# A hybrid convolution and state-space trunk: the input projection as a stage of its own, in seven block products

## The chip, the core and the metric

The kernel runs on one core of one Trainium2 chip. The metric is the device time of one execution in microseconds (us), lower is better. A core has a matrix engine (TensorE, PE in the profile; its weight loads are PEld), a vector engine (VectorE, DVE), an activation engine (ScalarE, ACT), GpSimd (POOL), and SyncE (SP), which here issues the transfers. The engines work on a memory on the chip with 128 partitions; matmul results go to an accumulator memory (PSUM) of eight banks of 512 float32 columns. Inputs, outputs and scratch tensors lie in device memory. Each engine runs its instructions in the order that was written for it.

## The reference

One layer over 1024 tokens of 1024 channels, all float32:

```python
h = layer_norm(x, ln_in_g, ln_in_b)
u = h @ w_in                      # 1024 x 9248 columns:
u_glu, z, xbc, dt_raw, gate_a, gate_b = split_in(u)
# u_glu 2x1024, z 2048, xbc 2048+2x512, dt 32, two gates of 1024
a, g = split(u_glu)
y_a = silu(layer_norm(causal_dwconv31(a * sigmoid(g)))) @ w_conv_out
xbc = silu(causal_dwconv4(xbc))   # x, B, C of the state-space scan
dt = softplus(dt_raw + dt_bias)
y = ssd_chunked(x, dt, -exp(a_log), B, C) + x * d_skip   # chunks of 128 tokens
y_b = rms_norm_by_group(y * silu(z)) @ w_ssm_out
mix = (sigmoid(gate_a) * y_a + sigmoid(gate_b) * y_b) @ w_o
h = layer_norm(ALPHA * h + mix)
gate, val = split(causal_dwconv3(h @ w_ffn_up))          # 2 x 2816 columns
h = layer_norm(ALPHA * h + (silu(gate) * val) @ w_ffn_down)
```

## The kernel before

Every matrix product is made of three float32r matmuls: both operands are split into a rounded part and a rest (`weights`, L144 to L153: ACT writes the rounded part at L149, DVE the rest at L150), and `mm3` adds rounded times rounded, rounded times rest and rest times rounded (L161 to L163). A tile of 128 columns over half of the tokens (512) and all 1024 input channels is `project`: eight k-steps of three matmuls, 24 in all, into one bank.

The tokens are worked on in two halves. For each half: `ln_in` normalises four row tiles of 128 tokens and transposes them to `hT`; `mixers` computes the projection columns and the two mixing branches; `combine` joins them; `out_proj` (for the second half `out_proj_pairs`) multiplies by `w_o` and applies the next LayerNorm.

`mixers` begins with the columns for dt and the first B and C (`first_columns`), turns dt into decays (`time_steps`), and then goes over four groups of heads. For a group it projects B, C and four x tiles with `conv4` on each (ACT copies the bank to `u`, one tap on ACT, three taps on DVE at L370, SiLU), computes z (`z_gate`, tokens on the partitions, L161 to L163 with `w_z`), projects the two GLU pairs of two channel tiles (`glu`), and runs the scan over four chunks of 128 tokens (`ssd_group`: transposes, the decay mask through POOL L473, PE L482, ACT L490 and L491 and DVE L507, the masked product L529, the state update). The 31-tap convolution of the two GLU tiles, 30 taps each on DVE at L415, is issued at a lower priority (`high_priority(offset=-1500)`). Small halo tiles carry the last tokens of the first half into the second. After the groups come the eight tiles of gate_a, kept in device memory; `combine` projects the eight tiles of gate_b in turn with the second half of the ssm output product (`w_sp`), does the LayerNorm of the convolution (`cc` to `sT`, POOL L611 to L624, DVE L618 to L631) and the product with `w_conv_out` (`w_co`).

The up projection works on all 1024 tokens at once, in a Winograd form of Strassen's scheme with seven block products for a pair of column tiles instead of eight. `ffn_blocks` forms the blocks and their sums from both halves of the tokens and of the channels. `up_first` computes the two products of the first tile that need only the first half of the tokens, for eight tiles ahead of the others and then interleaved with them, and keeps them in device memory; `up_rest` does the other five (12 matmuls each in `product`), and the weights' sums on DVE (`up_weights`, L823 to L829). The last stage is `down`.

The order on each engine is set by a list scheduler when the kernel is built: an instruction goes by program order shifted by the `offset` of the priority that it stands under, and by the time at which its inputs are expected; a tile waits until the buffer that it takes is free. Of the stages, tiles for weights have three buffers (`wst` for the loaded tile, `wsp` for its split), PSUM has four banks of kind `acc` (`bank(1)`) and four of kind `sm` (`bank(0)`), and two big tiles of 32 KB a partition hold hT, yT and mixT in turn.

Of the kernel before, what the change touches and what calls it, by code (L numbers as in the profile page):

```python
# [8 lines left out]
F32 = mybir.dt.float32  # L9
# [7 lines left out]
P = 128  # L17
D = 1024
# [10 lines left out]
EPS = 1e-5  # L29

# [25 lines left out]
def kernel(  # L56
# [37 lines left out]
    state_stack = ExitStack()  # L94
    statep = state_stack.enter_context(pool("states", side="right"))
    upper = statep.tile([P, P], F32, name="upper")
    make_upper_triangular(nc, upper, 1.0, diag=True)
    later = statep.tile([P, P], F32, name="later")
    make_lower_triangular(nc, later, 1.0, diag=False)
    ones = statep.tile([P, P], F32, name="ones")  # L100
    V.memset(ones, 1.0)
# [22 lines left out]
    a_log = statep.tile([P, HEADS], F32, name="a_log")  # L124
    dskip = statep.tile([P, HEADS], F32, name="dskip")
    u_halo = statep.tile([P, 24, 3], F32, name="u_halo")
    G.memset(u_halo, 0.0)
    v_halo = statep.tile([P, 8, KC - 1], F32, name="v_halo")
    G.memset(v_halo, 0.0)
    states = [statep.tile([P, HALF], F32, name=f"state{g}") for g in range(GROUPS)]  # L130
    dts = [statep.tile([P, 4, HEADS], F32, name=n) for n in ("dtv", "wds")]
    edc = statep.tile([P, 3, 4, HEADS], F32, name="edc")
    seg_mv = statep.tile([P, 4, P], F32, name="seg_mv")
    seg_st = statep.tile([P, 4, P], F32R, name="seg_st")
# [3 lines left out]
    first_scr = [dram.tile([2, P, HALF], F32, name=f"first_scr{j}") for j in range(NF)]  # L138
    act_scr = [dram.tile([P, T], F32, name=f"act_scr{j}") for j in range(NF)]
    c_scr = [dram.tile([8, P, HALF], F32, name=f"c_scr{i}") for i in range(2)]  # L140
    g_scr = [dram.tile([8, P, HALF], F32, name=f"g_scr{i}") for i in range(2)]
# [87 lines left out]
    def ln_in(hh):  # L229
        hT = big_tile(f"hT{hh}")  # L230
        with pool(f"lnin{hh}", side="right") as pl:
            first = hh == 0
            xts, gb = [], []
            with tc.high_priority(offset=6000):
                for t in range(4):
                    xt = pl.tile([P, D], F32, tag="x", bufs=4, name=f"x{hh}_{t}")
                    r0 = hh * HALF + t * P
                    SY.dma_start(xt, x[r0 : r0 + P, :])
                    xts.append(xt)
                    if first and t == 1:  # L240
                        gb = [row(pl, RW_ING, D, "in_g"), row(pl, RW_INB, D, "in_b")]
# [833 lines left out]
```

## Time and profile before

| | |
|---|---|
| time, median of 3 runs | 2039.81 us (2035.84 to 2040.16) |
| the profiled execution | 2041.08 us, its span 2039.3 us |
| mean granted TensorE clock | 0.996 |
| PE busy | 2000.0 us, 9296 matmul records |
| DVE busy | 1654.7 us, 2185 instructions |
| ACT / POOL busy | 973.0 us / 148.0 us |
| device memory | 279.81 MB moved, 137 GB/s on average |

"Busy" is the time in which at least one record of the engine was open. A matmul's record is longer than the distance to the next one, since matmuls overlap; so work on PE is priced by the distance between starts. Records on DVE overlap by some hundredths of a microsecond too. Rows of groups read: line, engine, operation, output from inputs, shapes, count, then busy time and the mean of one in ns, then idle time just before and what ended it. fp32 matmuls (the scan and the transposes) leave two records each.

### The profile page before, as it was taken

To read this page: it belongs to the slowest core of one execution; us is meant where nothing else is said; L and a number is where in the kernel's file an instruction comes from. 1 tells how busy PE (TensorE), PEld (TensorE's weight loads), DVE (VectorE), ACT (ScalarE), POOL (GpSimd) and SP (SyncE) were. 2 spreads that over 40 slices of the span, in tenths; PEclk is the share of its full clock that TensorE was granted. 3 is DMA by queue.
4 is the path that set the end of the run, shared out by engine and by line. 5 is a ranking of instruction groups with operands and counts; after the bars stand their busy time and mean duration, and the time that the engine had idled before them with its cause. 6 is when DMAs were issued, how large, how long until landed. Compare 5 with 4: busy or idle time off the path is not lost.

```text
span 2039.3 us, 24778 instructions
## 1 busy us (share of the span) xinstructions
PE 2000.0 (98%) x9296; PEld 1650.1 (81%) x9296; DVE 1654.7 (81%) x2185; ACT 973.0 (48%) x1392; POOL 148.0 (7%) x125
## 2 busy tenths in 40 slices
PE   7999999999999999999999999999999999999998
PEld 6888887888788888888888888877888888888886
DVE  7599999989766869999998976586888888853736
ACT  4465654556453356665454635354444444433231
POOL 2010101001400000100100130010000000000000
PEclk9999999999999999999999999999999999999999
DMA  6222223333436522222323353566454444464542
GB/s 218 93 69 88 86 94 104 99 103 114 158 121 213 209 88 77 90 84 76 126 88 104 109 171 128 195 217 217 155 164 157 164 165 156 160 227 149 209 159 83
DMA packets 95015, 279.81 MB, mean 137 GB/s; under 512 B 10800, under 2 KB 10800, under 8 KB 94896
## 3 DMA queue, kind: packets, MB, share of 16 engines
q1 hardware_dynamic: 94896, 278.24, 40.3%
q8 instruction: 73, 1.20, 0.2%
q14 instruction: 46, 0.38, 0.1%
HBM read 229.96 MB, written 48.23 MB: 136 GB/s over the span
## 4 chain that ended last, share of the span: by engine, by line
PE 69%; DVE 23%; issue 4%; DMA 2%; ACT 1%; SPq 0%; POOL 0%; DVEq 0%; ACTq 0%
PE acc L163 15%; PE acc L161 15%; PE acc L162 15%; DVE c L415 8%; PE sm L161 6%; PE sm L163 6%; PE sm L162 6%; DVE xbc L370 2%; PE acc L352 1%; PE sm L529 1%; PE sm L510 1%; DVE w_so L150 1%; DVE w_z L150 1%; DVE w_c L150 1%; PE sm L187 1%
## 5 line engine op out<-in xcount | busy, mean ns | idle before, releaser
L415 DVE SCALAR_TENSOR_TENSOR c<-v,pc,c 128x512 f32<-128x512 f32 x480 | 375.3, 805 | 7.2 <-ACT c L404 5.8
L473 POOL TENSOR_TENSOR au<-seg_mv,head_of 128x1024 fp32r<-128x1024 f32 x32 | 77.6, 2425 | 961.8 <-PE sm L482 728.8
L161 PE MATMUL acc<-hT,w_c 128*128 128x512 f32 x352 | 141.0, 400 | 0.0
L162 PE MATMUL acc<-hT,w_c 128*128 128x512 f32 x352 | 140.6, 399 | 0.0
L163 PE MATMUL acc<-hT,w_c 128*128 128x512 f32 x352 | 138.4, 393 | 0.0
L150 DVE TENSOR_TENSOR w_dn<-st_dn,w_dn 128x1024 fp32r<-128x1024 f32 x44 | 53.4, 1222 | 104.2 <-ACT w_dn L149 104.2
L370 DVE SCALAR_TENSOR_TENSOR xbc<-u,pc,xbc 128x512 f32<-128x512 f32 x144 | 109.8, 774 | 0.7 <-ACT xbc L368 0.5
L161 PE MATMUL sm<-h1s,w_s 128*128 128x512 f32 x264 | 103.5, 392 | 6.0 <-DVE fuv L848 3.1
L149 ACT CAST w_dn<-st_dn 128x1024 fp32r<-128x1024 f32 x44 | 46.0, 1053 | 131.6 <-PE sm L163 115.4
L162 PE MATMUL sm<-h1s,w_s 128*128 128x512 f32 x264 | 102.8, 389 | 0.0
L163 PE MATMUL sm<-h1s,w_s 128*128 128x512 f32 x264 | 102.1, 389 | 0.0
L162 PE MATMUL acc<-w_z,hT 128*128 128x512 f32 x256 | 100.8, 394 | 0.0
L161 PE MATMUL acc<-w_z,hT 128*128 128x512 f32 x256 | 100.8, 401 | 0.0
L163 PE MATMUL acc<-w_z,hT 128*128 128x512 f32 x256 | 100.7, 396 | 0.0
L149 ACT CAST w_c<-st_c 128x1024 fp32r<-128x1024 f32 x50 | 52.5, 1051 | 86.9 <-PE acc L163 66.2
L162 PEld LDWEIGHTS acc<-hT,w_c 128*128 128x128 f32 x352 | 66.1, 188 | 16.9 <-issue 3.8
L163 PEld LDWEIGHTS acc<-hT,w_c 128*128 128x128 f32 x352 | 66.1, 188 | 16.1 <-issue 2.6
L161 PEld LDWEIGHTS acc<-hT,w_c 128*128 128x128 f32 x352 | 66.1, 188 | 15.9 <-issue 2.6
L150 DVE TENSOR_TENSOR w_c<-st_c,w_c 128x1024 fp32r<-128x1024 f32 x47 | 60.6, 1289 | 20.2 <-ACT w_c L149 20.2
L163 PE MATMUL acc<-h1b,w_ue 128*128 128x512 f32 x176 | 68.5, 391 | 2.0 <-DVE w_ue L150 2.0
L161 PE MATMUL acc<-h1b,w_ue 128*128 128x512 f32 x176 | 68.7, 391 | 1.1 <-ACT s L807 0.7
L163 PE MATMUL sm<-h1b,w_s 128*128 128x512 f32 x176 | 69.2, 393 | 0.0
(312 smaller groups left out, 5741.8 us busy)
## 6 DMA issues: line engine op xcount, KB each, us to landing
st_c<-wcol SPq DMA_DIRECT2D x50, 512.0 KB, 3.5
st_dn<-wdown SPq DMA_DIRECT2D x44, 512.0 KB, 3.6
st_z<-wz SPq DMA_DIRECT2D x32, 512.0 KB, 3.4
st_wo<-wo SPq DMA_DIRECT2D x24, 512.0 KB, 3.9
st_ue<-wup SPq DMA_DIRECT2D x22, 512.0 KB, 4.1
ra<-wup SPq DMA_DIRECT2D x22, 512.0 KB, 3.8
rb<-wup SPq DMA_DIRECT2D x22, 512.0 KB, 3.5
act_scr<-fo SPq DMA_DIRECT2D x22, 512.0 KB, 2.7
```

What stands on the lines that cost most here:

```text
L149: A.copy(w[:, 0, :], st)
L150: (eng or V).tensor_tensor(out=w[:, 1, :], in0=st, in1=w[:, 0, :].bitcast(F32), op=ALU.subtract)
L161: TE.matmul(ps, wa(0), xa(0), start=start, stop=False, skip_group_check=more)
L162: TE.matmul(ps, wa(0), xa(1), start=False, stop=False, skip_group_check=more)
L163: TE.matmul(ps, wa(1), xa(0), start=False, stop=stop, skip_group_check=more)
L187: TE.transpose(pt[:, i * P : (i + 1) * P], src[:, (q + i) * P : (q + i + 1) * P], ident)
L352: TE.matmul(ps[:, ts], w[:, i, k * P : (k + 1) * P], hT[:, j, k, ts], start=n == 0 and k == 0, stop=n == 2 and k == KD - 1,)
L370: V.scalar_tensor_tensor(out=o, in0=u[:, k : k + HALF], scalar=pc[:, wc + k : wc + k + 1], in1=o, op0=ALU.mult, op1=ALU.add,)
L415: V.scalar_tensor_tensor(out=accs[i], in0=v[:, k : k + HALF], scalar=pc[:, wc + k : wc + k + 1], in1=accs[i], op0=ALU.mult, op1=ALU.add,)
L473: G.tensor_tensor(out=au, in0=seg_mv[:, c, :].unsqueeze(1).to_broadcast([P, 8, P]), in1=head_of[:, g, :].unsqueeze(2).to_broadcast([P, 8, P]),
L510: TE.matmul(po, CT[:, cs], S, start=True, stop=True)
L529: TE.matmul(py[:, hs], m[:, h, :], xs[:, hs], start=True, stop=True)
```

## The change

The columns of the input projection, all but z, are taken out of `mixers` and `combine` and computed over all tokens before the mixers, in the seven-product form of the up projection. `ln_in` is replaced by `in_blocks`, which normalises all eight row tiles and forms the blocks; `blocks` holds what `ffn_blocks` did. `columns` first computes the two early products of eight pairs (`lead_first`), closes the pool of the rows, and then goes over 28 pairs in a written order (GLU pairs, x, B with C, gates); `pair` computes a pair, and its convolution, GLU or sigmoid follows. The results, `xbc`, `v` and both gates over 1024 tokens, go to device memory, and the dt columns too (`time_columns`, five block products of 12). The 31-tap convolution of the first half of the tokens is done there; that of the second half is issued after the first mixers at an offset of -1500. The mixers read their tiles back. The blocks' first tile `b1` serves as `hT` for z of the first half; for the second, `rebuild` reads the normalised rows and transposes them. The tiles of the scan's states are opened only after the columns (`open_states`). The up projection uses the same `pair`: the first eight are led, the others compute all seven products in a row, with copies on ACT in place of some additions on DVE. The pair's loaded weights come from `wst` and no longer from a pool of their own.

```diff
-    def ln_in(hh):
...
-    def column(hh, hT, ct):
...
-    def first_columns(hh, hT, cts):
...
-    def time_steps(pl, hh, ps):
+    def time_steps(pl, hh):
         dtc = pl.tile([HEADS, HALF], F32, tag="yo", name=f"dtc{hh}")
-        A.activation(
-            out=dtc, in_=ps[:HEADS, :], func=AF.Identity, bias=pc[:HEADS, PC_DTB : PC_DTB + 1]
-        )
+        SY.dma_start(dtc, dt_scr[:, hh * HALF : (hh + 1) * HALF])
...
-    def conv4(pl, hh, ps, j):
+    def conv4(pl, j, u):
+        o = pl.tile([P, T], F32, tag="o", bufs=2, name=f"xo{j}")
...
+        A.activation(
+            out=o, in_=u[:, U0 : U0 + T], func=AF.Identity, scale=pc[:, wc + 3 : wc + 4]
+        )
         for k in range(3):
             V.scalar_tensor_tensor(
                 out=o,
-                in0=u[:, k : k + HALF],
+                in0=u[:, U0 - 3 + k : U0 - 3 + k + T],
...
+        SY.dma_start(xbc_scr[j], o)
+    def glu(i, ua, ug):
+        a, g = ua[:, U0 : U0 + T], ug[:, U0 : U0 + T]
+        A.activation(out=g, in_=g, func=AF.Sigmoid)
+        V.tensor_mul(a, a, g)
+        SY.dma_start(v_scr[i], a)
...
     def mixers(hh, hT):
-        pre = first_columns(hh, hT, (CT_DT, CT_B, CT_C))
         with pool(f"mixers{hh}") as pl:
-            time_steps(pl, hh, pre[0])
+            time_steps(pl, hh)
             for g in range(GROUPS):
...
+                tiles = []
+                for j in (*range(4 * g, 4 * g + 4), 16 + g, 20 + g):
+                    o = pl.tile([P, HALF], F32, tag="xbc", bufs=12, name=f"xbc{hh}_{j}")
+                    SY.dma_start(o, xbc_scr[j][:, hh * HALF : (hh + 1) * HALF])
+                    tiles.append(o)
                 zs = z_gate(pl, hh, hT, g)
-                vs = [(i, glu(pl, hh, hT, i)) for i in (2 * g, 2 * g + 1)]
-                done = ssd_group(pl, hh, g, xT, BT, CT, zs)
+                done = ssd_group(pl, hh, g, tiles[:4], *tiles[4:], zs)
...
+    def lead_first(qp, bl, js, src, n=1):
+        ws = {j: weights(src(j), f"ue{j}") for j in js}
+        pss = {j: bank(1) for j in js}
+        for h in range(n):
+            ts = slice(h * HALF // n, (h + 1) * HALF // n)
+            for q, block in enumerate(("b11", "b21")):
+                for j in js:
+                    product(
...
+                    for t in range(ts.start, ts.stop, HALF // 2):
+                        f = qp.tile([P, HALF // 2], F32, tag="f", bufs=4, name=f"f{j}{q}{t}")
+                        A.copy(f, pss[j][:, t : t + HALF // 2])
+                        SY.dma_start(first_scr[j][q][:, t : t + HALF // 2], f)
+    def pair(upp, bl, j, src_a, src_b):
+        led = j < LEAD
         with tc.high_priority(offset=2000):
+            r1 = wst.tile([P, D], F32, tag="st", name=f"ra{j}")
+            SY.dma_start(r1, src_a)
+            r2 = wst.tile([P, D], F32, tag="st", name=f"rb{j}")
+            SY.dma_start(r2, src_b)
+            ue = None if led else split_pair(wsp, r1, f"ue{j}")
...
+        ps, pz = bank(1), bank(0)
+        if led:
+            SY.dma_start(s, first_scr[j][0])
+            SY.dma_start(ua[:, e], first_scr[j][1])
+            product(ps, lambda i: w24[:, i, :HALF], bl["t2"], True)
+            V.tensor_tensor(out=u2, in0=s, in1=ps, op=ALU.add)
+            product(pz, lambda i: w3[:, i], bl["t3"], True)
+            product(ps, lambda i: w10[:, i, :HALF], bl["t1"], False)
+            V.tensor_tensor(out=ub[:, l], in0=s, in1=ps, op=ALU.add)
+        else:
+            product(ps, lambda i: ue[:, i, :HALF], bl["b11"], True)
+            A.copy(s, ps)
+            py = bank(1)
+            product(py, lambda i: ue[:, i, HALF:], bl["b21"], True)
+            V.tensor_tensor(out=ua[:, e], in0=s, in1=py, op=ALU.add)
+            product(ps, lambda i: w24[:, i, :HALF], bl["t2"], False)
+            A.copy(u2, ps)
+            product(pz, lambda i: w3[:, i], bl["t3"], True)
+            product(ps, lambda i: w10[:, i, :HALF], bl["t1"], False)
+            A.copy(ub[:, l], ps)
+        V.tensor_tensor(out=ub[:, l], in0=ub[:, l], in1=pz, op=ALU.add)
+        product(pz, lambda i: w10[:, i, HALF:], bl["t4"], False)
+        V.tensor_tensor(out=ub[:, e], in0=u2, in1=pz, op=ALU.add)
+        product(ps, lambda i: w24[:, i, HALF:], bl["b22"], False)
...
+    def columns(bl, tp_stack, qp):
...
+        for r in range(4):
+            order += [glus[2 * r], xs[2 * r], bcs[r], gates[2 * r], xs[2 * r + 1]]
+            order += [glus[2 * r + 1], gates[2 * r + 1]]
...
+        lead_first(qp, bl, range(3), first, 2)
+        for j in range(3, LEAD):
+            lead_first(qp, bl, (j,), first)
+        tp_stack.close()
+        with pool("columns") as pl:
+            for j, (kind_, i) in enumerate(order):
+                ua, ub = pair(pl, bl, j, wcol[srcs[j][0]], wcol[srcs[j][1]])
+                if kind_ == "g":
+                    glu(i, ua, ub)
+                    with tc.high_priority(offset=-300):
+                        conv31(pl, 0, (i,))
...
+                if j == LEAD:
+                    time_columns(pl, bl)
...
-    hT = ln_in(0)
-    yT = mixers(0, hT)
-    mixT = combine(0, hT, yT)
-    hT = ln_in(1)
+    bl = in_blocks(tp_stack.enter_context(pool("intrans")), qp)
+    columns(bl, tp_stack, qp)
+    in_stack.close()
+    open_states()
+    cvp = state_stack.enter_context(pool("conv", side="right"))
+    yT = mixers(0, bl["b1"])
+    with tc.high_priority(offset=-1500):
+        for i in range(0, 8, 2):
+            conv31(cvp, 1, (i, i + 1))
+    mixT = combine(0, yT)
+    hT = rebuild(1)
...
-    LEAD = 8
-    firsts_to(LEAD)
+    for j in range(LEAD):
+        lead_first(qp, bl, (j,), lambda j: wup[j])
...
     for j in range(NF):
-        firsts_to(LEAD + (j + 1) * (NF - LEAD) // (NF - 1))
-        up_rest(upp, bl, j)
+        up(upp, bl, j)
```

385 lines of the change are left out of this document (190 added, 195 removed).

## The prediction

> **What bounds the kernel now.** I read the page first, then the table of busy time by stretch, then the order of time on PE and DVE inside the stretches, and last the groups of instructions.
>
> ```profile
> span 2039.3 us, 24778 instructions
> PE 2000.0 (98%) x9296; PEld 1650.1 (81%) x9296; DVE 1654.7 (81%) x2185; ACT 973.0 (48%) x1392; POOL 148.0 (7%) x125
> ```
>
> PE idles 39 us of 2039, so PE work taken away is the only large thing to win. DVE is the next engine, with 385 us spare over the whole run. Where that spare time lies is in the stretches (columns: stretch, its length, busy time and count of PE, PEld, DVE, ACT, POOL, then the granted clock, the DMA share and GB/s):
>
> ```profile
> 0.00:39.00 39.00, 26.16 (x181) 25.22 (x182) 28.48 (x44) 14.21 (x29) 10.85 (x15) 1.00 0.70 242
> 39.00:500.00 461.00, 460.06 (x2185) 377.48 (x2186) 424.94 (x591) 265.50 (x424) 38.96 (x16) 1.00 0.29 94
> 500.00:691.00 191.00, 185.80 (x833) 152.84 (x832) 133.65 (x173) 77.39 (x103) 22.49 (x14) 0.98 0.50 171
> 691.00:1192.00 501.00, 500.54 (x2448) 414.20 (x2448) 463.62 (x647) 274.91 (x417) 38.62 (x16) 1.00 0.30 99
> 1192.00:1308.00 116.00, 115.44 (x505) 94.55 (x505) 73.61 (x86) 53.33 (x68) 22.41 (x14) 1.00 0.45 151
> 1410.00:1800.00 390.00, 386.93 (x1696) 318.83 (x1695) 334.53 (x387) 163.33 (x179) 4.08 (x41) 1.00 0.48 160
> 2015.00:2040.00 25.00, 15.25 (x68) 12.30 (x66) 21.01 (x40) 1.18 (x4) 0.00 (x0) 0.90 0.23 84
> ...
> 1003.00:1045.00 42.00, 41.54 (x200) 33.62 (x199) 42.00 (x57) 16.89 (x30) 4.81 (x3) 1.00 0.30 99
> ```
>
> 39 to 500 is mixers of the first half of the tokens, 691 to 1192 mixers of the second, 1192 to 1308 the second combine, 1410 to 1800 the up projection. In the two mixers PE is full, but DVE is already busy 92% (425 of 461, 464 of 501), and for a while all the time (42.00 of 42). The projection columns are what keeps PE full there, while DVE does the scan and the 31-tap convolution under them. The change takes exactly those columns out of there.
>
> **Prices.** Records overlap, so prices are start to start.
>
> ```profile
> 1542.58 0.39 PE L161 MATMUL acc<-h1b,w_ue 128*128 128x512 f32 x1
> ...
> 1545.07 0.39 PE L163 MATMUL acc<-h1b,w_ue 128*128 128x512 f32 x1
> ```
> ```profile
> 450.87 1.21 DVE L150 TENSOR_TENSOR w_gt<-st_gt,w_gt 128x1024 fp32r<-128x1024 f32 x1
> 452.00 2.73 DVE L415 SCALAR_TENSOR_TENSOR c<-v,pc,c 128x512 f32<-128x512 f32 x4
> 454.65 0.68 DVE L530 TENSOR_TENSOR t<-t,sm 128x512 f32<-128x512 f32 x1
> 455.25 0.68 DVE L495 TENSOR_TENSOR xs<-sm,dtv 128x512 f32<-128x512 f32 x1
> ...
> 1539.70 1.28 DVE L863 SCALAR_TENSOR_TENSOR fo<-fuv,pc,fo 128x1024 f32<-128x1024 f32 x1
> 1540.90 0.69 DVE L727 TENSOR_TENSOR w_s<-s,w_s 128x512 fp32r<-128x512 f32 x1
> ```
> ```profile
> 788.62 1.73 PE sm L529 x16
> ```
>
> A matmul of 512 columns costs 2.49/11 = 0.226 us. On DVE a weight split of 1024 costs 1.13, a tap 2.65/4 = 0.66, a tensor operation of 512 costs 0.60, a tap of 1024 costs 1.20. The eight fp32 products of a chunk (from the chain, two records each) take 1.73, so 0.11 a record.
>
> **The work, before and after.** PE: 57 column tiles, two halves, 24 matmuls each were 2736. Now 28 pairs of 84 and 60 for the time steps are 2412: 324 fewer, 73 us. rebuild adds 32 transposes of two records each, 7 us at 0.11. Net 66 us off PE. DVE: a pair needs three splits of 1.13 and five half-wide operations of 0.60, 6.4 us, where two tiles in two halves needed four splits, 4.5: 53 us more over the 28. Putting blocks together costs five operations of 0.60 in the 8 led pairs and three in the other 20: 60 us. The block sums of four token rows, seven operations each, 18 us. conv4 in 1024 instead of 512 saves 12. DVE ends some 85 us up, PE 66 down; over the whole run PE (1934) still leads DVE (1740), so all hangs on the stages.
>
> **A, to the end of the eight lead products.** By the first stretch, PE had done three columns at 39; five more leads are 5x24x0.226 = 27, so 66. DVE must after 39 normalise and split four more rows (each two operations of 1.20, two of 0.60 and small ones, 4.0, and seven of 0.60 for the sums, 4.2: 33 in all), do five lead splits (5.7) and the first pair's weights (5.3): about 45, so 84. The first led product needs the sums of all four late rows. I take 83; the ends are 66 and 95.
>
> **B, the columns.** PE: 8x60+20x84+60 = 2220 matmuls, 503 us. DVE: weights 171, blocks 60, conv4 72x1.20 = 86, GLU 9, half of the taps 240x0.66 = 158 (POOL has next to nothing here): 484. PE leads, as in the up stage with the same products (386.93 of 390): 507. A new wait stands in `pair`: the t4 product adds to bank pz, which DVE must have read first, and it follows t1 directly, where the b22 product stood between; behind it on PE's queue stand b22 and the next pair. The nearest row is
>
> ```profile
> L161 PE MATMUL sm<-h1s,w_s 128*128 128x512 f32 x264 | 103.5, 392 | 6.0 <-DVE fuv L848 3.1
> ```
>
> 6 us of idling in the whole up stage. The cover is the next pair's first product; with it the cost is nothing or below (the order may even pack better), without it a copy and an addition, about 2x0.60 us, in each of 20 pairs, 24. I take the row's 6: B is 513.
>
> **C to E, mixers, combine with out_proj, mixers.** Here are no columns any more. The rows of 691 to 1192 give what leaves:
>
> ```profile
> L415 DVE SCALAR_TENSOR_TENSOR c<-v,pc,c 128x512 f32<-128x512 f32 x240 | 187.6, 806 | 3.4 <-ACT c L404 2.7
> L370 DVE SCALAR_TENSOR_TENSOR xbc<-u,pc,xbc 128x512 f32<-128x512 f32 x72 | 53.9, 763 | 0.6 <-ACT xbc L368 0.5
> L150 DVE TENSOR_TENSOR w_c<-st_c,w_c 128x1024 fp32r<-128x1024 f32 x23 | 29.7, 1291 | 7.1 <-ACT w_c L149 7.1
> L150 DVE TENSOR_TENSOR w_gg<-st_gg,w_gg 128x1024 fp32r<-128x1024 f32 x8 | 9.7, 1217 | 8.4 <-ACT w_gg L149 8.4
> ...
> L162 PE MATMUL acc<-hT,w_c 128*128 128x512 f32 x176 | 70.8, 402 | 0.0
> L352 PE MATMUL acc<-hT,w_c 128*128 128x256 f32 x144 | 17.4, 283 | 0.0
> L162 PE MATMUL acc<-hT,w_gb 128*128 128x512 f32 x16 | 6.3, 394 | 0.0
> L162 PE MATMUL acc<-yT,w_sp 128*128 128x512 f32 x13 | 5.1, 389 | 0.0
> ```
>
> PE of one mixers: 500.5 less (3x176 + 576 + 48 + 39) x 0.226 (576: the 24 tiles of w_ga, w_gg, w_gt) less 17 is 213. Between the two lie sp, co and wo, 576 matmuls, and the 7 us of rebuild: 137. Together 563. DVE: 463.6 less taps (240x(0.806-0.08), the overlap, is 174), conv4 49, w_c 28, three groups like w_gg 27, and some 33 small ones (GLU, gb, sp, the end of out_proj) 23, is 162 for each mixers. 500 to 691 has 133.7; 15 taps, 8 splits, four rows of the input LayerNorm and the scan's end, some 48, leave it, 12 of out_proj come back: 98. The second half's convolution must now fit in here too: 174. Sum 162+98+162+174 = 596, over PE's 563. DVE sets this part. At the share it has in the mixers now (0.92) this would be 648, at the share of its fullest stretch 600; since the taps are a filler that waits for nothing, I take 0.96: 621.
>
> What else could set it is the scan's chain, and the way into it:
>
> ```profile
> L259 ACT ACTIVATE dtc<-acc,pc x2: 673/675/677, 35.0 to 710.0; 32x512 f32<-32x512 f32 x2
> L473 POOL TENSOR_TENSOR au<-seg_mv,head_of x32: 1897/2342/3892, 69.7 to 1139.7; 128x1024 fp32r<-128x1024 f32 x32
> ...
> 1159.82 0.60 ACT L490 ACTIVATE m<-sm 128x512 f32<-128x512 f32 x1
> 1161.04 1.28 ACT L491 ACT_TABLE_LOAD   x1
> 1162.33 0.63 ACT L491 ACTIVATE m<-m 128x512 f32<-128x512 f32 x1
> ...
> L507 DVE TENSOR_TENSOR m<-m,cbm x32: 1206/1214/1226, 112.5 to 1163.0; 128x1024 f32<-128x1024 f32 x32
> ```
>
> time_steps takes 35 us (35.0 to 69.7); z of two groups, 2x96x0.226 = 43, lies over it. A chunk with one buffer for m costs two relus, a table load, two exps, the mask and L529, some 8 us with the hand-overs; 16 chunks are 130, under a mixers' share of the 621. So the chain is covered, unless queues stretch a chunk to 13 us.
>
> **F, the second combine.**
>
> ```profile
> L194 DVE TENSOR_TENSOR yT<-sm,yT x32: 671/682/692, 197.1 to 1186.1; 128x512 fp32r<-128x512 f32 x32
> L178 DVE TENSOR_TENSOR sT<-cc,sT x16: 684/690/693, 572.3 to 1251.1; 128x512 fp32r<-128x512 f32 x16
> ```
>
> From the last yT to the last sT, the convolution's LayerNorm took 65 us under sp and gb products, 87 us of PE. Without gb only sp's 43 cover it. I give the chain 57 without gb's splits beside it (ends 43 and 65), then co's 43: 100, where 1186 to 1308 were 122. So a gain of 22, though the matmuls taken away were 43.
>
> **G, the rest.** Now all eight led pairs of the up stage come in a row: DVE 5.3+3.0+4x1.20+1.20 = 14.3 each against 60x0.226 = 13.6 on PE, where first products of later tiles stood between. At 0.96 that is 119 instead of 109: 10 more (ends 0 and 25, the t4 wait). Transfers: wcol is read once instead of twice, xbc, v and gates go out and in; at DMA shares of 0.29 to 0.50 I price both at nothing; if their cover is gone, a group's start waits some 4 us. The input's zero columns, constants and open_states lie beside other work and cost nothing that I can see, up to 5 where the state tiles wait for the last pair.
>
> **Sum.** 83+513+621+100 = 1317 where 1308 stood: 9 more; with G 19 more. The profiled execution took 2041.1 for its span of 2039.3; 2060 in its terms, and the median of the runs is 1.3 below it: 2059.
>
> **Rivals.** *PE stays the bound, faster.* For it: under 97 to 100% DVE PE loses next to nothing (1003 to 1045). Against: this held for 42 us, not 600. Then A is 75, B 503, C to E 600, F 95, G 3: 1273+3 against 1308, 32 less: 2008. It decides where C to E needs under some 610 with B near 505. At the extreme, with all 66 us, 1974.
>
> *The mixers become a chain, slower still.* For it: under 16 chunks lie only z and ssm_out_first, 576 matmuls or 130 us, where 1191 more lay; one buffer each for au, m, xs, yo ties chunk to chunk, and taps queue ahead of each step. Against: greedy filling has kept PE at 100% there. From 13 us per chunk it decides; at 14, two mixers are 2x(224+30) and 150 between: 658, 37 more than my 621. PE would then idle within each chunk, and the last stretch shows what follows: idle for 10 of 25 us, the granted clock falls to 0.90, 2.5 us lost; 0.8 in each of 32 chunks is 25 more. 2059+62 = 2121. [...]
>
> **Numbers.** The forecast, DVE setting C to E, has 0.48, with 2036 to 2088 as its own range; the faster rival 0.33, the chain 0.19. What can be told from no change here is 0.2%, 4 us: faster 0.33, within it 0.07 (the forecast's lower edge), slower 0.60. The range 1990 to 2115 takes in the faster rival's price and nearly the chain's; under 2 in 10 stay outside.
>
> **What would show it.** Right: PE near 1934 busy; DVE over 95% from about 600 to 1220 with taps the filler and PE at 90%; PE waits at co products on sT; first led pairs of both stages waiting for DVE. Wrong: the second yT before 1195 (the faster rival), or chunks of L529 over 13 us apart with both PE and DVE idle and a clock below 1.00 (the chain); PE waiting for DVE at t4 in every pair would make B 530 and over.

## The result, and the profile after

The changed kernel takes 2313.41 us (median of 4 runs, 2308.45 to 2314.73) where the kernel before takes 2039.99 (2035.84 to 2041.78): 1.134 times as long, 95% interval 1.1315 to 1.1364. The forecast was 2059, with a range from 1990 to 2115.

These are the first lines of the page after, with the rows of the slices for PE, DVE and the granted clock.

```profile
span 2313.0 us, 24397 instructions
...
PE 2056.2 (89%) x8932; PEld 1648.2 (71%) x8932; DVE 1767.4 (76%) x2320; ACT 950.1 (41%) x1318; POOL 144.6 (6%) x191
...
PE   6989999999945778889997699889988999999998
...
DVE  8798978989799899877465676767787777773635
...
PEclk9989999999977878989998898899998999999999
```

PE has 364 instructions fewer than before and is yet 56 us longer busy. DVE is 113 longer busy, and no engine is full over the whole run. The slices 12 to 27 (some 640 to 1560 us) hold the loss: PE at 4 to 9 tenths and, in the same slices, a clock of 7 to 9.

The table of busy time by stretch (same columns as before) gives the stages. First the columns stage:

```profile
81.00:134.00 53.00, 46.90 (x190) 37.22 (x189) 40.92 (x56) 17.50 (x18) 0.40 (x4) 0.94 0.39 125
134.00:300.00 166.00, 151.83 (x626) 120.08 (x625) 153.44 (x199) 64.40 (x72) 1.97 (x19) 0.96 0.35 115
300.00:500.00 200.00, 196.16 (x857) 159.82 (x856) 165.22 (x207) 99.04 (x119) 2.25 (x22) 1.00 0.32 112
500.00:634.00 134.00, 129.64 (x561) 105.72 (x561) 116.68 (x148) 62.95 (x75) 2.33 (x19) 0.99 0.32 111
```

Then from its last product to the last yT: the way into the first mixers (to its first au), the first mixers (to its last yT), combine and out_proj up to the second mixers' first au, the second mixers; and last what follows combine(1).

```profile
633.00:737.00 104.00, 57.91 (x223) 46.12 (x221) 101.87 (x166) 24.21 (x32) 0.06 (x1) 0.73 0.32 107
737.00:1016.00 279.00, 213.04 (x917) 158.90 (x918) 255.06 (x358) 114.38 (x189) 44.55 (x23) 0.83 0.23 73
1016.00:1211.00 195.00, 184.91 (x806) 151.02 (x804) 120.98 (x171) 71.45 (x96) 11.55 (x8) 0.95 0.50 166
1211.00:1465.00 254.00, 206.56 (x919) 157.55 (x919) 159.31 (x215) 108.39 (x180) 42.51 (x23) 0.86 0.22 72
...
1561.00:2313.00 752.00, 721.76 (x3148) 589.29 (x3146) 517.53 (x620) 305.45 (x398) 13.74 (x50) 0.98 0.41 139
```

| stage | forecast | after |
|---|---|---|
| A, to the first product with a sum of blocks (the last lead product starts at 78.2) | 83 | 81 |
| B, columns | 513 | 553 |
| C to E, to the last yT | 621 | 831 |
| F, second combine | 100 | 97 |
| the rest | 741 (before 731, and 10) | 752 |

So 210 of the 254 us between forecast and result lie in C to E, 40 in B, 11 in the rest. What is to be seen in C to E: the first 383 us have DVE full (357 busy, 0.93), the last 254 have neither DVE (0.63) nor PE (0.81) full. One stretch thus looks like the forecast's mechanism and the other like the chain rival's.

**The way in.** The timeline of DVE and of SP's queue, and two rows of the waits in 634 to 737:

```profile
654.55 33.87 DVE L368 SCALAR_TENSOR_TENSOR c<-v,pc,c 128x512 f32<-128x512 f32 x51
688.34 0.17 DVE L255 TENSOR_SCALAR sp<-a_log 128x32 f32<-128x32 f32 x1
688.43 8.03 DVE L368 SCALAR_TENSOR_TENSOR c<-v,pc,c 128x512 f32<-128x512 f32 x12
696.39 0.28 DVE L256 COPY sp<-sm 128x128 f32<-128x128 f32 x1
```
```profile
685.79 0.33 SPq L377 DMA_DIRECT2D c_scr<-c  x1
686.17 0.42 SPq L241 DMA_DIRECT2D dtc<-dt_scr  x1
686.64 2.99 SPq L515 DMA_DIRECT2D xbc<-xbc_scr  x6
```
```profile
PE sm L244 <- DMA dtc<-dt_scr: 26.0, 1, 26.0
...
SPq L377 <- DVE c L368: 31.1, 2, 30.8
```

time_steps can't begin before dtc is loaded. The load stands on SP's queue behind the store of the last c tile, which waits 30.8 us for taps (L368). (The mixers' tiles also take the memory of the columns' pool, in which that c tile lies; e3 takes both away at once, so the queue and the memory weren't told apart.) DVE does 51 taps in a row, then 12 more, before the first step that uses dtc, at 696.39. From 634 to 1016 start 264 taps (120 in the way in, 144 in the mixers), so 24 were left of the first half, and the others here are the second half's, which nothing needs before the second combine. The first au starts at 737.

**A chunk.** The timeline of PE in a chunk of the second mixers, where there is not one tap:

```profile
1237.29 1.12 PE L463 MATMUL sm<-state,xbc 128*128 128x512 f32 x2 [0.43 <-ACT m L443]
1242.18 0.80 PE L170 MATMUL acc<-w_z,hT 128*128 128x512 f32 x1 [3.76 <-ACT zs L396]
1242.77 0.63 PE L171 MATMUL acc<-w_z,hT 128*128 128x512 f32 x1
...
1247.89 0.46 PE L171 MATMUL acc<-w_z,hT 128*128 128x512 f32 x1
...
1248.66 0.40 PE L171 MATMUL acc<-w_z,hT 128*128 128x512 f32 x1
1248.90 0.40 PE L172 MATMUL acc<-w_z,hT 128*128 128x512 f32 x1
1249.13 1.02 PE L471 MATMUL sm<-xsd,bt 128*128 128x512 f32 x2
```

Between two steps of the chunk (L463 and L471) 18 z products of a later group stand in PE's order. They wait 3.76 us for the Silu of an earlier z (L396), which empties their bank; twelve of them then run 5.12/12 = 0.43 us apart, where 0.24 is seen at the end and 0.226 was the price before. So work that was to fill PE's idle time lies in the chain, and at half speed.

### The profile page after: what moved, and what is told of

The parts are those of the page before. It is cut to its first block, busy times and chain, and to the rows that moved or that the text cites. A ratio compares the mean times of both kernels' runs of the same rounds, so it can differ in the third digit from the quotient of the medians.

```text
span 2313.0 us, 24397 instructions
## 1 busy us (share of the span) xinstructions
PE 2056.2 (89%) x8932; PEld 1648.2 (71%) x8932; DVE 1767.4 (76%) x2320; ACT 950.1 (41%) x1318; POOL 144.6 (6%) x191
## 4 chain that ended last, share of the span: by engine, by line
PE 62%; DVE 24%; ACT 5%; DMA 4%; issue 4%; POOL 0%; SPq 0%; DVEq 0%; ACTq 0%; POOLq 0%
PE acc L170 15%; PE acc L172 15%; PE acc L171 15%; DVE c L368 9%; PE sm L172 4%; PE sm L170 4%; PE sm L171 4%; PE sm L482 2%; DVE w_s L668 2%; DVE xo L326 1%; DMA rb<-wcol 1%; DVE t L492 1%; DVE t L484 1%; DVE fo L946 1%; DMA v<-v_scr 1%
## 5 line engine op out<-in xcount | busy, mean ns | idle before, releaser
L368 DVE SCALAR_TENSOR_TENSOR c<-v,pc,c 128x512 f32<-128x512 f32 x480 | 357.1, 772 | 18.5 <-ACT c L357 16.8
L170 PE MATMUL acc<-hs,w_s 128*128 128x512 f32 x336 | 136.8, 407 | 17.0 <-ACT ub L859 6.2
L172 PE MATMUL acc<-hs,w_s 128*128 128x512 f32 x336 | 133.8, 402 | 4.9 <-DVE w_s L668 4.9
L171 PE MATMUL acc<-hs,w_s 128*128 128x512 f32 x336 | 134.8, 401 | 0.0
L667 ACT CAST w_s<-rb 128x1024 fp32r<-128x1024 f32 x50 | 52.7, 1054 | 147.8 <-PE acc L172 111.7
L172 PE MATMUL acc<-h1s,w_s 128*128 128x512 f32 x264 | 105.6, 403 | 7.8 <-DVE w_s L668 7.8
L170 PE MATMUL acc<-h1s,w_s 128*128 128x512 f32 x264 | 106.2, 402 | 6.7 <-ACT w_s L667 4.5
L443 ACT ACTIVATE m<-sm 128x512 f32<-128x512 f32 x64 | 36.3, 594 | 174.2 <-PE sm L435 174.0
L171 PE MATMUL acc<-h1s,w_s 128*128 128x512 f32 x264 | 105.4, 399 | 0.0
L170 PE MATMUL acc<-hb,w_ue 128*128 128x512 f32 (+1 forms) x248 | 92.7, 375 | 5.6 <-ACT w_ue L667 2.4
L171 PE MATMUL acc<-hb,w_ue 128*128 128x512 f32 (+1 forms) x248 | 91.9, 371 | 0.0
L482 PEld LDWEIGHTS sm<-xs,m 128*128 128x128 f32 x512 | 71.0, 217 | 29.1 <-issue 16.4
L170 PEld LDWEIGHTS acc<-hs,w_s 128*128 128x128 f32 x336 | 65.3, 194 | 37.2 <-ACT ub L859 8.9
L170 PE MATMUL sm<-hb,w_s 128*128 128x512 f32 x224 | 87.6, 391 | 1.9 <-ACT w_s L667 1.9
L172 PE MATMUL acc<-hb,w_ue 128*128 128x512 f32 (+1 forms) x248 | 88.4, 372 | 0.9 <-DVE w_ue L668 0.9
L172 PE MATMUL sm<-hb,w_s 128*128 128x512 f32 x224 | 87.3, 391 | 0.2 <-DVE w_s L668 0.2
L171 PE MATMUL sm<-hb,w_s 128*128 128x512 f32 x224 | 87.4, 390 | 0.0
L482 PE MATMUL sm<-xs,m 128*128 128x64 f32 x512 | 70.9, 299 | 12.8 <-DVE m L460 12.7
L172 PEld LDWEIGHTS acc<-hs,w_s 128*128 128x128 f32 x336 | 65.6, 195 | 20.6 <-DVE w_s L668 6.4
```

The lines of the kernel that those rows point to most:

```text
L170: TE.matmul(ps, wa(0), xa(0), start=start, stop=False, skip_group_check=more)
L171: TE.matmul(ps, wa(0), xa(1), start=False, stop=False, skip_group_check=more)
L172: TE.matmul(ps, wa(1), xa(0), start=False, stop=stop, skip_group_check=more)
L368: V.scalar_tensor_tensor(out=accs[i], in0=v[:, k : k + HALF], scalar=pc[:, wc + k : wc + k + 1], in1=accs[i], op0=ALU.mult, op1=ALU.add,)
L443: A.activation(out=mq, in_=pg, func=AF.Relu)
L482: TE.matmul(py[:, hs], m[:, h, :], xs[:, hs], start=True, stop=True)
```

## The experiments

The stages of every run (us; *way in* to *rest* as cut above, *columns end* is the last columns product) and its time beside that of the kernel before on the same chip:

| run | columns end | way in | mixers 1st | between | mixers 2nd | F | rest | median | ratio, 95% |
|---|---|---|---|---|---|---|---|---|---|
| after | 634 | 103 | 279 | 195 | 254 | 97 | 752 | 2313.4 | 1.1315-1.1364 |
| e1_no_taps2 | 631 | 56 | 258 | 196 | 256 | 94 | 750 | 2245.0 | 1.0997-1.1032 |
| e2_taps_late | 631 | 52 | 259 | 244 | 260 | 96 | 755 | 2292.3 | 1.1221-1.1261 |
| e3_own_conv | 633 | 64 | 296 | 197 | 257 | 95 | 752 | 2291.9 | 1.1221-1.1268 |
| e4_gates_back | 500 | 132 | 299 | 228 | 271 | 129 | 750 | 2308.0 | 1.1308-1.1342 |
| e5_zs8 | 630 | 109 | 268 | 194 | 235 | 96 | 748 | 2290.1 | 1.1194-1.1250 |
| e6_no_taps1 | 612 | 64 | 290 | 195 | 256 | 95 | 752 | 2260.6 | 1.1063-1.1100 |
| e7_zs8_conv | 633 | 73 | 278 | 198 | 239 | 96 | 752 | 2270.5 | 1.1117-1.1150 |
| e8_up_before | 632 | 103 | 280 | 195 | 251 | 96 | 732 | 2287.4 | 1.1182-1.1246 |
| e9_scan_alone | 627 | 83 | 255 | 180 | 191 | 96 | 752 | 2180.3 | 1.0657-1.0725 |
| e10_no_silu | 630 | 103 | 273 | 195 | 244 | 97 | 752 | 2294.7 | 1.1229-1.1274 |
| e11_scan2 | 632 | 103 | 281 | 194 | 252 | 95 | 752 | 2310.3 | 1.1312-1.1350 |
| e12_warm | 630 | 73 | 289 | 195 | 246 | 94 | 756 | 2283.0 | 1.1178-1.1211 |
| e13_parts | 629 | 54 | 271 | 194 | 269 | 95 | 727 | 2246.3 | 1.1011-1.1050 |
| e14_parts_scan2 | 632 | 52 | 272 | 195 | 266 | 94 | 727 | 2241.1 | 1.0982-1.1017 |
| e15_alone_warm2 | 626 | 82 | 260 | 178 | 176 | 95 | 751 | 2168.6 | 1.0619-1.0680 |
| e16_alone_warm4 | 629 | 82 | 268 | 178 | 206 | 95 | 751 | 2210.7 | 1.0825-1.0888 |

Two explanations stood at the start: T, taps stand ahead of the scan's steps in DVE's order; G, too little PE work is left under the scan.

**e1_no_taps2**

```
-        for k in range(KC - 1):
+        for k in range(KC - 1 if hh == 0 else 0):
```

> Leaves out the 240 DVE taps of the second half's 31-tap convolution (its ACT tap, loads and stores stay). Theory T (taps stand ahead of the first scan's steps on DVE's in-order queue): the stretch from the last columns product to the end of the first mixers, 104 + 277 = 381 us after, falls to 285 or less, which is what the second mixers takes without a tap (35 + 250); whole kernel 2313 to about 2190-2215. Theory G (the gaps come from too little PE work under the scan and the clock that falls in them, taps are harmless fillers): that stretch stays over 350 and the kernel over 2280. In both the second mixers stays at some 285, 72 over its PE work of 213.

The way in fell by 47, the first mixers by 21: together 314, neither 285 nor 350, and the kernel came out between the two answers as well. These are its two mixers by busy time:

```profile
687.00:945.00 258.00, 206.32 (x922) 157.19 (x923) 158.16 (x214) 108.18 (x184) 42.23 (x23) 0.86 0.21 71
1141.00:1398.00 257.00, 207.42 (x922) 157.34 (x921) 161.24 (x215) 108.32 (x180) 42.63 (x23) 0.85 0.22 71
```

T is right for the way in. Within the mixers taps aren't the first cause: without one, each takes 257, with DVE busy for 160 of it.

**e2_taps_late**

```
-    cvp = state_stack.enter_context(pool("conv", side="right"))
     yT = mixers(0, bl["b1"])
+    cv_stack = ExitStack()
+    cvp = cv_stack.enter_context(pool("conv"))
```

> Same work; the second half's convolution gets its buffers out of the memory that the first mixers frees, so none of its taps can run before combine(0). T: the first mixers with the way into it falls from 381 to about 285, the second grows from 285, by as much of the 240 taps (158 us) as does not fit under combine(0) and out_proj, where DVE has 58 us to spare: 60 to 100 more; in sum 2313 to about 2285-2320. G: neither stretch moves by more than 20.

As T had it in direction and in the whole time: way in and first mixers are those of e1, 311 together (T had 285), and the taps come back further on. They do so mainly in *between* (244, with DVE busy 232), where they now stand ahead of the second time_steps.

**e3_own_conv**

```
-                        conv31(pl, 0, (i,))
+                        conv31(cvp, 0, (i,))
```

(`cvp` is opened ahead of the columns' pool, and serves both halves.)

> Same work; one pool of convolution buffers for both halves, opened before the columns stage and kept, so that the columns' pool is free when its last pair is done and the load of dtc need not stand behind the last c tile's taps and store on SP's queue. T: the first au comes at about 690 instead of 738, the kernel gains 30 to 50: 2265-2285. If the stretch is set by PE's lack of work (G) the kernel moves by less than 15.

The first au came at 697, and the way in lost 39. But the first mixers took 17 more, since the taps that no longer ran ahead of it now run in it: 22 won, less than the 30 to 50 expected.

**e4_gates_back**

```
+            for j in range(8):
+                pg = bank(1)
+                project(pg, weights(wcol[CT_GA + j], f"gt{hh}_{j}"), hT)
...
+                project(pg, weights(wcol[CT_GB + j], f"gb{hh}_{j}"), hT)
```

(The 8 "t" pairs leave the order of the columns.)

> The 16 gate columns go back to where they were before the change (ga at the end of each mixers, gb in combine, 24 matmuls a tile and half); the columns stage keeps glu, x, B, C and the time steps, 20 pairs instead of 28. Columns stage 553 less 8x84x0.226 = 152: 401. G: the 768 matmuls (174 us) run in the gaps and keep the clock up, the stretch C to E comes down from 828 to 760 or so; kernel about 2090. T: taps still stand in the scan's way, gates only fill under it, C to E 830 to 860; kernel 2160-2190.

Both missed. The columns ended 134 earlier, and nearly all of it was spent: 29 in the way in, 19 and 33 in the first mixers and what follows, 18 and 32 in the second mixers and the combine behind it. The way in shows why for its part:

```profile
500.00:631.00 131.00, 50.37 (x216) 40.94 (x214) 125.55 (x201) 26.87 (x35) 0.00 (x0) 0.69 0.30 97
```

A shorter columns stage leaves more of the taps for the way in (157 instead of 120), and DVE does them first. The ga products, 192 x 0.226 = 43 us in each mixers, cost 18 to 19 there; the gb products cost some 32 in each combine, where PE was nearly full. G in its simple form falls: 174 us of PE work put back did not go into idle time for nothing.

**e5_zs8**

```
-            z = pl.tile([P, HALF], F32, tag="zs", bufs=5, name=f"zs{hh}_{g}_{t}")
+            z = pl.tile([P, HALF], F32, tag="zs", bufs=8, name=f"zs{hh}_{g}_{t}")
```

> Same work; zs gets 8 buffers (two groups) instead of 5. In the runs so far a group of four chunks takes some 64 us in both mixers, with taps or without, with gate products under it or without. Theory Z: between the state matmuls of a chunk PE's in-order queue holds 12 to 24 ssm_out or z products whose acc bank still holds the last group's z; that bank is emptied by a Silu that waits for a zs buffer, which the chunk's own t*zs frees. So the products are in the chain instead of beside it. With 8 buffers the wait of acc on zs goes (4 us a chunk now) and the pace falls to 50 or less a group; both mixers together 60 to 100 shorter, kernel 2215-2255. Rival R: the pace comes from the single buffers of m, au and xs and the hand-overs; it stays at 60 or more and the kernel within 15 of 2313.

The second group of the second mixers fell from 64.4 to 50.0, as expected, but the third stayed at 62.4 (63.1). The two mixers lost 30 together instead of 60 to 100, and the kernel 23; the profiled execution is the fastest of the run's four (2280.6), so the 30 may be some us too many. The z banks are one cause, and not the largest.

**e6_no_taps1**

```
-        for k in range(KC - 1):
+        for k in range(KC - 1 if hh else 0):
```

> Leaves out the 240 DVE taps of the first half's 31-tap convolution (second half's stay). If DVE's share in the columns stage (0.9 in its first 215 us, with led pairs and taps together) made it 553 instead of 513, the stage falls to 510-520; if the raw weights' three buffers or the t4 wait did, it stays over 540. Way into the first mixers 104: down to some 80, since the second half's taps still stand ahead there. Kernel 2313 to about 2250 in the first case, 2290 in the second.

The columns ended at 612, a stage of 531, between the two answers: 22 of the 40 us too many are taps. The way in fell to 64, more than expected. Two stretches of the stage, after and then here:

```profile
134.00:200.00 66.00, 56.97 (x219) 44.27 (x218) 60.13 (x77) 25.37 (x25) 0.82 (x8) 0.90 0.45 152
200.00:300.00 100.00, 94.86 (x409) 75.81 (x408) 93.30 (x123) 39.03 (x47) 1.15 (x11) 1.00 0.28 91
```
```profile
134.00:200.00 66.00, 59.57 (x248) 47.16 (x249) 51.71 (x63) 28.31 (x29) 0.93 (x9) 0.97 0.51 170
200.00:300.00 100.00, 100.00 (x443) 82.81 (x442) 55.48 (x63) 42.11 (x51) 1.12 (x11) 1.00 0.30 102
```

Without taps PE is full from 200 to 500. Up to 200, in the led pairs, it still isn't: it idles 11 us there, and 5 more after 500. What of the other 18 us is DVE and what the three raw buffers wasn't tried.

**e7_zs8_conv**, the edits of e5 and e3 together.

> e5 and e3 together (8 zs buffers; one pool of convolution buffers opened before the columns). Two separate causes add: e5's gain and 20 more. If the way into the scan and the scan's pace share one cause (taps on DVE), less than e5's gain alone plus 10.

43 less than after, where e5 alone brought 23 and e3 alone 22. So they are separate losses.

**e8_up_before**: `up` and `lead_first` of the up projection replaced by the functions before the change.

```
-    for j in range(LEAD):
-        lead_first(qp, bl, (j,), lambda j: wup[j])
+    firsts_to(LEAD)
...
-        up(upp, bl, j)
+        firsts_to(LEAD + (j + 1) * (NF - LEAD) // (NF - 1))
+        up_rest(upp, bl, j)
```

> The up projection as it was before the change (first products of tile 8 and on spread between the other tiles, own raw buffers, the old order t2 t1 t3 b22 t4); all else as after. From the end of combine(1) to the end stood 731 before and 752 after: if the led pairs in a row make the 21, the kernel gains 15 to 25, 2288-2298; if the tail is longer for another reason, within 6.

The rest is 732 again, and the kernel gains 26. So the 21 lost behind combine(1) come from the new form of the up projection (order, led pairs and buffers were put back together and weren't told apart).

**e9_scan_alone**

```
-        pss = [bank(1) for _ in range(4)]
...
-            A.activation(out=z, in_=pss[t], func=AF.Silu)
+            G.memset(z, 1.0)
...
-            project(ps, w, yT)
```

> Leaves out the z products and the ssm_out_first products (zs and ya are filled with constants by POOL), so that the mixers hold the scan and the taps alone; 1152 matmuls (260 us of PE) less. Theory Q (PE's queue is in order, and z and so blocks stand between the steps of a chunk and lengthen it instead of lying beside it): the chain by itself is some 9.5 us a chunk, the second mixers falls from 254 to 155-175, the first from 279 to 180-215 (taps). Rival R (the chain itself is 15 us, by hand-overs and single buffers): the second mixers stays over 225.

```profile
710.00:965.00 255.00, 159.31 (x550) 108.78 (x551) 248.29 (x371) 74.31 (x142) 45.38 (x38) 0.61 0.13 45
1145.00:1336.00 191.00, 133.98 (x547) 96.65 (x548) 142.19 (x200) 67.31 (x135) 51.09 (x42) 0.73 0.15 49
```

191 lies between the two answers. The scan with little else on PE takes 191/16 = 11.9 us a chunk in the second mixers. With z and ssm_out_first it is 254: the 372 PE instructions more (919 against 547), 84 us at 0.226, cost 63. That is not PE's price alone: with the products go their Silus, 11 of the table loads on ACT, and the splits of their weights, and by e10 some 10 of the 63 us are the loads. So at most three quarters of the 84 us of PE work lie in the scan's way; what the splits take of the 63 wasn't tried. In the first mixers the taps alone do what z and so do: 255 with DVE busy for 248.

The 11.9 is a mean of two things. Inside a group of four chunks the sixteen products of L470 (L482 in the changed kernel) start 7.1 to 11.3 us after those of the chunk before, some 9 on average; from the last chunk of a group to the first of the next it is 18.7 to 23.4. PE at such an end of a group:

```profile
1221.53 3.65 PE L470 MATMUL sm<-xs,m 128*128 128x64 f32 x16 [2.45 <-DVE m L448]
1230.18 3.67 PE L196 MATMUL sm<-ident,t 128*128 128x128 f32 x16 [5.00 <-DVE t L480]
1233.65 1.05 PE L408 MATMUL sm<-ident,xbc 128*128 128x128 f32 x4
```

The transposes of the finished group (L196) stand on PE's queue ahead of the next group's first ones (L408), and wait 5.00 us for its normalisation. In the changed kernel the chunks of the second mixers' first three groups start mostly 14 to 16 us apart, and those of the last group, with no z left between their steps, 8.8 to 11.2.

**e10_no_silu**

```
-            A.activation(out=z, in_=pss[t], func=AF.Silu)
+            A.activation(out=z, in_=pss[t], func=AF.Relu)
```

> Leaves out the sigmoid in z's Silu (Relu instead), which takes away ACT's table loads between Exp and Silu, 18 and 19 loads of 1.28 us in each mixers after. If they lie in the chunk's chain: about 15 to 22 less in each mixers, kernel 2270-2283. If they lie beside it: within 8 of 2313.

6 and 10 less in the mixers, 19 in the whole kernel: neither within 8 nor 15 to 22 a mixers. The loads fell from 19 and 18 to 7 and 7, 30 us less of ACT; 16 of these 30 us, about half, lay in the chain.

**e11_scan2**

```
-            au = pl.tile([P, 8, P], F32R, tag="au", name=f"au{nm}")
+            au = pl.tile([P, 8, P], F32R, tag="au", bufs=2, name=f"au{nm}")
```

(and the same for m, xs and xsd)

> Same work; two buffers instead of one for au, m, xs and xsd, so that a chunk can begin under the one before. Rival R (single buffers set the pace): a group falls from 64 to 50-55, both mixers 60 to 100 shorter, 2215-2255. Theory Q: the order on PE and the z banks set it; within 20 of 2313.

Within 4 us of after, so single buffers don't set the pace. Only the first groups, whose z stands ready, fell (from 49 to 34 and from 42 to 29).

**e12_warm**

```
+                for k in range(2):
+                    TE.matmul(pg, hT[:, 0, k, :P], hT[:, 0, k, :], start=True, stop=True)
```

(and six into `py`)

> As e7 (2270), with idle products added into banks that are overwritten after: two before each of a chunk's two seg matmuls and six before the state matmuls L482, 320 in all, 72 us of PE at the full clock. Theory K (a good part of the scan's slowness is PE at half clock after each wait, matmuls 0.45 apart instead of 0.226, L482 3.5 instead of 1.73): the added work keeps the clock up and the kernel is not slower than e7, 2235-2270. If the clock doesn't matter the added products stand in the chain: 2290-2335.

13 slower than e7 for 72 us of added work: between the answers, and so no verdict.

**e13_parts** and **e14_parts_scan2**: e5 and e8 together, with the second half's convolution moved into the mixers; the second adds the buffers of e11.

```
-            part = pl.tile([P, HALF], F32, tag="ya", bufs=2, name=f"sp_part{hh}")
+            part = pl.tile([P, HALF], F32, tag="c", bufs=2, name=f"sp_part{hh}")
...
+                with tc.high_priority(offset=-1500):
+                    if g in (0, 1):
+                        i = 4 * hh + 2 * g
+                        conv31(pl, 1, (i, i + 1))
```

> Full work. Takes three named losses away together: zs has 8 buffers; the up projection is as before the change; the second half's convolution stands half in each mixers, its c tiles sharing two buffers with time_steps' last tiles, so that no tap of it can precede time_steps. If the losses are separate they add: way into the scan 103 to 52 (-50), first mixers 279 to 245-255, second 254 to 240-250, up -20; kernel 2205-2230. If they share one cause (DVE's total, or the chain alone), 2245 or more.

> As e13_parts, with two buffers for au, m, xs and xsd as in e11 (xbc 9 buffers instead of 12 for the room). In e11 a group whose z products were already done fell from 42-49 to 29-34, the others stayed at 64 behind the z banks. If the banks were what held them, with zs 8 a group comes to 45-52 and the kernel to 60-90 under e13. If the chain of hand-overs through the four small PSUM banks holds them, within 20 of e13.

```profile
629.00:682.00 53.00, 48.03 (x210) 39.18 (x209) 38.95 (x67) 22.12 (x29) 0.00 (x0) 0.94 0.56 191
682.00:954.00 272.00, 209.47 (x926) 160.12 (x925) 236.86 (x336) 107.28 (x184) 45.93 (x23) 0.81 0.23 73
...
1148.00:1417.00 269.00, 205.91 (x920) 159.89 (x919) 238.32 (x336) 106.37 (x179) 44.45 (x23) 0.82 0.23 74
```

The way in (54) and the rest (727) came as expected, so both are separate losses. The mixers didn't: in the second, 120 taps cost 34 over e5's 235, and in the first, 120 instead of e5's 141 brought nothing (271 against 268). e14 is within 20 of e13: the double buffers, which failed alone, fail with 8 zs buffers too. What holds the groups at 65 to 78 with all these buffers isn't settled. Left are the four small PSUM banks, of which a chunk allocates seven, the order of PE's queue, and the taps themselves, since DVE is busy for 237 of 272 and 238 of 269 us in these two mixers; none of the three was tried by itself with all buffers in place.

**e15_alone_warm2** and **e16_alone_warm4**: e9 with idle products, 12 and 24 a chunk.

> As e9 (the scan and the taps alone, z and ssm_out_first left out), with idle products of 512 columns added into banks that are overwritten after: two before each seg, state-out and state-in matmul and four before L482's sixteen, 12 a chunk, 2.7 us of PE at full clock. In e9 the chunk 1239 to 1247 took 8.1 us with L482 at 1.97, the next two 9.6 to 10.6 with L482 at 3.6, and the granted clock stood at 0.72. Theory K (the gaps of the chain halve PE's clock, and its steps then take twice as long): groups two and three of the second mixers fall from 44.5 and 46.9 to 38-43, the second mixers from 191 to 170-185, with more work done. Without K the added 2.7 us a chunk show: 200-230.

> As e15 with twice as many idle products, 24 a chunk, 5.4 us of PE at full clock: K: clock near 1.0, L482 at 1.73, but the products no longer all fit in the waits; second mixers 175-200. Without K 230 and over.

The second mixers of the one and of the other:

```profile
1145.00:1321.00 176.00, 143.56 (x726) 108.78 (x727) 141.13 (x201) 70.02 (x135) 50.31 (x42) 0.90 0.16 53
```
```profile
1157.00:1363.00 206.00, 181.77 (x910) 144.98 (x909) 139.55 (x201) 68.52 (x135) 52.49 (x42) 0.93 0.13 45
```

With 184 idle products more in these 16 chunks (the last chunk of a group has two fewer), 42 us of PE, the mixers is 15 us shorter: 176 instead of 191, the clock 0.90 instead of 0.73. That is inside K's 170 to 185. Groups two and three came to 42.1 and 41.3. Chunk by chunk, the sixteen products of these two groups start 8.0, 10.6, 7.1 and 7.9, 10.7, 9.6 apart in e9 and 7.7, 8.1, 7.5 in both groups here: the long chunks are gone, as K has it. The size is less sure than the direction, for there are two executions of each, and those of e9 lie 11 us apart with the longer one profiled; the whole kernel is 6 to 17 us shorter, with such products in both mixers. Twice as many no longer fit in the waits: 206, over K's 200 and under the 230 without K.

## Why the prediction was wrong

**A and F** came within 5 and 3 us of their terms. (The terms for DVE's added work, 53, 60, 18 and less 12, make 119 and not the 85 written; DVE was busy 113 us longer. The stages were summed separately, so the forecast doesn't rest on it.)

**B.** The sum of DVE's work was right (484; measured 476, with 24 taps or 16 us left over for later). The step that failed is "PE leads, as in the up stage with the same products": that stage has no 31-tap convolution beside it. e6 shows that the taps made 22 of the 40. The 6 us for the new t4 wait were aimed at the wrong place. This group of the page after holds the first matmul of each set of three in the t3 and t4 products:

```profile
L170 PE MATMUL sm<-hb,w_s 128*128 128x512 f32 x224 | 87.6, 391 | 1.9 <-ACT w_s L667 1.9
```

It idled 1.9 us in the whole stage, and for weights. PE idles 28 us in the stage, 20 of them before 300, where the led pairs are (to 209) and DVE is fullest.

**C to E**, 621 forecast, 831 measured. The two sums were less wrong than their use: DVE needed 637 instead of 596 (24 taps of the first half came over from the columns, 16 us at 0.66), and PE was busy 662 instead of 563. Most of these 99 us are products at a lower clock: PE's busy time in the four stretches, each times its granted clock, is 572. The first step that failed is the next one, "since the taps are a filler that waits for nothing, I take 0.96". This filler was put first: the taps went in at the beginning, 264 of them in 383 us, where DVE was full at 0.93 and the scan stood behind them, and in the 449 us after that DVE was busy for 280, with no tap left. That is the smaller part. In e2, where the taps come later, C to E is still 815, and in e1, with none of these 240 taps, 766: 145 of the 210 us too many stay.

The step that cost more is "So the chain is covered", and two covers failed. time_steps' 35 us were to lie under z of two groups, 43; the way in took 103, for the taps and the dtc load stood ahead of time_steps (e1, e2 and e13: 52 to 56 without). And a chunk was priced at "some 8 us with the hand-overs", 16 of them at 130. For the bare chunk inside a group that was nearly right (some 9 in e9). The sum had no term for the end of a group, 10 us or more each time, and none for z's products between a chunk's steps: alone the scan takes 191, or 11.9 a chunk (e9), with z and so between its steps 253.8/16 = 15.9, with the taps too 279.1/16 = 17.4.

**The chain rival**, given 0.19, was the right mechanism. Its condition, 13 us a chunk, is met (15.9 and 17.4), and its sign, chunks with PE and DVE idle under a clock below 1.00, is what 1211 to 1465 shows. Its price, 62, was too small in three terms: 14 us a chunk (17.4 and 15.9), 30 for the way into each mixers (the first 103), and 25 for the clock (99 us more of PE, not all of it in the chain). The 25 was read from the last stretch before, 2015 to 2040, and there no product lost time: the granted clock is 1.00 up to 2035.0, PE's last product starts at 2029.86, and only behind that, with PE idle, does the clock fall (0.50 from 2036.0 to 2039.3). The ground taken against it, "greedy filling has kept PE at 100% there", was read from a kernel in which PE was the bound: there a chunk had some 25 us (a group's first au starts at 69.7, the next at 169.2 and 270.4), and the trace before doesn't show what it needed.

The rows on the clock in the second mixers:

```profile
1424.96 1.02 PE L463 MATMUL sm<-state,xbc 128*128 128x512 f32 x2
1428.68 1.85 PE L471 MATMUL sm<-xsd,bt 128*128 128x512 f32 x2 [2.69 <-ACT bt L459]
1430.32 3.52 PE L482 MATMUL sm<-xs,m 128*128 128x64 f32 x16
```

In the chunk before, at 1421.07, the sixteen records of L482 take 1.89 us; here, behind a wait of 2.69, they take 3.52, and the granted clock is 1.00 from 1424.9 to 1428.6 and 0.50 from 1429.0 to 1435.0. Above, behind the 3.76 us that z waited, the products come 0.43 apart, and the granted clock is 0.50 from 1241.5 to 1248.0. In e9 slow products stand behind a wait of 2.00 (last section). How long a wait has to be for it was not tried.

**G.** 21 instead of 10, inside its ends 0 to 25; e8 puts it on the up projection's new form.

**The faster rival** needed C to E under 610; nothing came near.

## What to carry to other kernels

When a change takes the bounding engine's work out of a stage, ask first what the dependent chain of that stage needs by itself, with that engine idle, the ends of its groups included. A stage that was full gives only an upper bound of it (here 25 us a chunk were available, 12 are needed alone, 16 to 17 with the filler that is left). Work that waits for nothing wasn't free here: it was put ahead of the steps that matter, on DVE (51 taps in a row, 33.87 us, ahead of time_steps) and on SP's queue (the dtc load behind a store that waited 30.8 us), so bound its place by a dependence, as e13 did for the way in. And price a thin stage at the clock that it is granted (0.83 and 0.86 in the two mixers here, 0.73 in the way in).

## What was not expected of the hardware

A chain was shorter with more work in it: 42 us of idle products on PE went with a mixers of 176 instead of 191, and a granted clock of 0.90 instead of 0.73 (e9, e15; two executions each). And slow products stand behind a wait of 2.00 us as well. This is PE in e9, in which L459 stands for L471 and L470 for L482:

```profile
1239.06 1.12 PE L459 MATMUL sm<-xsd,bt 128*128 128x512 f32 x2 [1.98 <-ACT bt L447]
1240.25 1.97 PE L470 MATMUL sm<-xs,m 128*128 128x64 f32 x16
...
1247.06 1.13 PE L459 MATMUL sm<-xsd,bt 128*128 128x512 f32 x2 [2.00 <-ACT bt L447]
1248.18 3.61 PE L470 MATMUL sm<-xs,m 128*128 128x64 f32 x16
```

No wait in these rows is over 2.00. Behind the one of 1.98 the sixteen products take 1.97 us, behind the one of 2.00 they take 3.61, 1.8 times as long; the granted clock of 1217 to 1264 is 0.72. What makes the difference the rows don't show.
